# Masked maxima of the scores ahead of the keys' additions on VectorE, and all probabilities scaled on ScalarE

## The chip, the cores and the metric

One core of one Trainium2 chip runs the whole program. The metric is device time in microseconds (us) of one execution; smaller is better. The kernel before took 485.41 us, the median of three runs (484.21 to 485.72).

## The reference

A decoder trunk of two layers over 256 tokens with 1024 channels, all in float32. Layer 0 mixes tokens by attention with 8 heads of 128 channels; at 256 tokens there is one key block, so it is plain causal attention. Layer 1 mixes them by causal pooling. Each layer is followed by a squared-ReLU MLP with 4096 hidden channels, and a last RMSNorm closes the trunk.

```python
qkv = (xn @ w_qkv).reshape(b, s, 3, N_HEADS, HEAD_DIM)
q = apply_partial_rope(q, cos, sin)          # the first 32 channels of each head
k = apply_partial_rope(k, cos, sin)
s_own = jnp.einsum('bhqd,bhkd->bhqk', qc, k_own) * scale
s_own = jnp.where(kpos[None, :] <= qpos[:, None], s_own, NEG_INF)
p = jax.nn.softmax(s_own, axis=-1)
out = einsum('bhqk,bhkd->bhqd', p, v) @ w_o
x = x + out
x = x + squared_relu_mlp(rms_norm(x, norm_mlp[i]), w_up, w_down)   # relu(x @ w_up)**2 @ w_down
```

## The kernel before

Weights arrive from memory in slabs of 1 MB, `slabs`, in the order of their use: values, then keys and queries of two heads in turn, the output projection, and the MLP. Every slab is split into a high and a low part of reduced width: ScalarE copies the high part (`hi`, L177), VectorE subtracts it from the slab (`lo`, L181, "the split"). Most slabs have two pieces of 128 x 1024. The splits run about three slabs ahead of their use, and calls such as `pump_h(1)` and `pump(1)` place them among the other work. Products are then made of three matrix products of parts, summed in PSUM.

The order of work on every engine is written out by hand: an engine executes its instructions in the order in which the program gives them, and an instruction that waits holds all behind it on its engine.

The attention stage runs over `j`, pairs of heads, from 0 to 3 (L716 to L756). For `j` of 1 to 3, TensorE makes the keys of pair `j` in two banks (`wide_lo`, then `attend(j - 2)`, then `wide_hi`), then the scores of pair `j - 1` (L636, L637), then the queries of pair `j` (L410 to L415, some 5.9 us), then transposes the probabilities of pair `j - 1` (`prob_t`, L670). So each of these three blocks holds on the other engines:

- `key_evac` (L609): for both heads ScalarE copies the half of the bank with the small terms (L615) and VectorE adds the other half (L616, "the additions"); VectorE shuffles the 32 rotary channels (L617); GpSimd does the rotation in three operations (L620, L621, L622).
- `scores` (L629): VectorE adds the causal mask to each piece of the scores and takes the maximum of it in one instruction (L640, "the maxima": two pieces for each of the two heads); ScalarE makes a high part (L177) and then the four exponentials with their sums (L648); VectorE makes one split and then the reciprocals of the four sums (L651); then the probabilities are scaled, the first head's two pieces on ScalarE (L656), the second head's two on VectorE (L659).
- `qk_evac` (L593): VectorE shuffles (L598) and multiplies (L599) the queries; the rest is on VectorE for `j` = 1 and on GpSimd for `j` = 2 and 3 (L601, L602).
- `attend(j - 2)` (L688): the attention output of an earlier pair is copied by ScalarE (L709) and its low part is made by VectorE (L710).

The scores of pair 3 have no keys beside them: `scores(3)` stands among the output projection (L773).

The scores, transposed probabilities and attention outputs share one ring of two PSUM banks (`ps_t`, tag "t"). In the order of allocation, the second head's scores of pairs 1, 2 and 3 (`s_1_1`, `s_2_1`, `s_3_1`) come to the bank that the attention output of pair 0, 1 and 2 (`o_0`, `o_1`, `o_2`) had. TensorE therefore can't load for these scores before L710 of that pair has read the bank.

Of the kernel before, what the change touches and what calls it, by code (L numbers as in the profile page):

```python
# [11 lines left out]
F32 = mybir.dt.float32  # L12
F32R = mybir.dt.float32r
I32 = mybir.dt.int32
AF = mybir.ActivationFunctionType
ALU = mybir.AluOpType
ENG = mybir.EngineType

P = 128
SEQ = 256  # L20
# [64 lines left out]
def tile_trunk(ctx: ExitStack, tc: tile.TileContext, x_in, positions, norm_mix, norm_mlp,  # L85
               w_qkv, w_o, pool_w, pool_scale, w_up, w_down, norm_final, consts, out):
    nc = tc.nc
# [5 lines left out]
    work = ctx.enter_context(tc.tile_pool(name="work", bufs=2))  # L93
# [93 lines left out]
    def hi_step():  # L187

        if not todo:
            i = state["next"]  # L190
            if i > min(state["cur"] + AHEAD, len(slabs) - 1):
                return False
            todo.extend(split_steps(i))
            state["next"] += 1
        step = todo.pop(0)
        step[0]()
        lows.append((state["next"] - 1, not todo, step[1]))
        return True
# [11 lines left out]
    def pump_h(n):  # L210
        for _ in range(n):
            hi_step()

    def pump_l(n):
        for _ in range(n):
            lo_step()
# [7 lines left out]
    def use(kind, j, pieces=99):  # L224

        i = index[(kind, j)]
        state["cur"] = max(state["cur"], i)
        while done.get(i, 0) < pieces:
            if not lo_step():
                hi_step()  # L230
        wh, wl = halves[i]
        kk = slabs[i][1].shape[1]
        return (wh.rearrange("p (k f) -> p k f", k=kk), wl.rearrange("p (k f) -> p k f", k=kk))
# [184 lines left out]
    def chan_block(acc, w, f):  # L418
        for k in range(KT):
            chan_hi(acc, w, k, f, k == 0)  # L420
            chan_lo(acc, w, k, f, k == KT - 1)

    def wide_lo(acc, w, k, f, first=True):

        nc.tensor.matmul(acc[:, 0:SEQ], w[1][:, k, f * P:(f + 1) * P], xs[:, k, 0:SEQ],  # L425
                         start=first and k == 0, stop=not first and k == KT - 1,
                         skip_group_check=True)
# [79 lines left out]
    for k in range(KT):  # L507
# [29 lines left out]
        if 2 <= k < 6:  # L537
# [3 lines left out]
                                 scale=1.0 / 32.0, accum_out=acc0[:, h, s:s + 1])  # L541
        if k == 5:
# [4 lines left out]
                                           op0=ALU.add, op1=ALU.add)  # L547
# [22 lines left out]
    def v_evac(s, h):  # L570
        nc.scalar.activation(vsb[:, s, h * HALF:(h + 1) * HALF], dv[s, h], AF.Copy, scale=r0[s])
# [5 lines left out]
    scale = 1.0 / math.sqrt(P)  # L577
    tab = {}

    def tables():  # L580
        for nm, c in (("k", 1.0), ("q", scale)):
            ct = cpool.tile([P, 1, SEQ], F32, name="ct_" + nm)
            st = cpool.tile([ROT, 1, SEQ], F32, name="st_" + nm)
            nc.vector.scalar_tensor_tensor(ct[:, 0, :], rb[:, 0:SEQ], c, cos_t, op0=ALU.mult, op1=ALU.mult)
            nc.vector.scalar_tensor_tensor(st[:, 0, :], rb[0:ROT, 0:SEQ], c, sin_t, op0=ALU.mult, op1=ALU.mult)
            tab[nm] = (ct, st)
# [3 lines left out]
    def qk_bank(nm, j):  # L590
        return ps_u.tile([P, HALF], F32, tag="u", name="u_%s_%d" % (nm, j))

    def qk_evac(nm, j, u):  # L593
        ct, st = tab[nm]
        t = work.tile([P, 2, SEQ], F32, tag="X", name="t_%s_%d" % (nm, j), bufs=4)
        sw = work.tile([ROT, 2, SEQ], F32, tag="sw", name="sw_%s_%d" % (nm, j), bufs=2)
        uv = u.rearrange("p (f t) -> p f t", f=2)
        nc.vector.stream_shuffle(sw.rearrange("p f t -> p (f t)"), u[0:ROT, :], swap)  # L598
        nc.vector.tensor_tensor(t, uv, ct.broadcast_to([P, 2, SEQ]), op=ALU.mult)  # L599
        e = nc.vector if j == 0 or (nm, j) == ("q", 1) else nc.gpsimd  # L600
        e.tensor_tensor(sw, sw, st.broadcast_to([ROT, 2, SEQ]), op=ALU.mult)  # L601
        e.tensor_tensor(t[0:ROT], t[0:ROT], sw, op=ALU.add)  # L602
        return t

    def key_banks(j):
        return [ps_d.tile([P, HALF], F32, tag="d%d%d" % (f, 1 - j % 2), name="k_%d_%d" % (j, f))
                for f in range(2)]

    def key_evac(j, us):  # L609

        ct, st = tab["k"]
        t = work.tile([P, 2, SEQ], F32, tag="X", name="t_k_%d" % j, bufs=4)
        sw = work.tile([ROT, 2, SEQ], F32, tag="sw", name="sw_k_%d" % j, bufs=2)
        for f in range(2):
            nc.scalar.activation(t[:, f, :], us[f][:, SEQ:2 * SEQ], AF.Copy)  # L615
            nc.vector.tensor_tensor(t[:, f, :], us[f][:, 0:SEQ], t[:, f, :], op=ALU.add)  # L616
        nc.vector.stream_shuffle(sw.rearrange("p f t -> p (f t)"),  # L617
                                 t[0:ROT].rearrange("p f t -> p (f t)"), swap)
        e = nc.gpsimd
        e.tensor_tensor(t, t, ct.broadcast_to([P, 2, SEQ]), op=ALU.mult)  # L620
        e.tensor_tensor(sw, sw, st.broadcast_to([ROT, 2, SEQ]), op=ALU.mult)  # L621
        e.tensor_tensor(t[0:ROT], t[0:ROT], sw, op=ALU.add)  # L622
        return t

    qk = {}
    prob = {}
    mask = cst[:, C_MASK:C_MASK + 3 * P]

    def scores(j):  # L629
        q, k = qk["q", j], qk["k", j]  # L630
        pr = []
        mx = small.tile([P, 4], F32, tag="mx", name="mx_%d" % j)
        sums = small.tile([P, 4], F32, tag="sums", name="sums_%d" % j)
        for a in range(2):
            sp = ps_t.tile([P, HALF], F32, tag="t", name="s_%d_%d" % (j, a))
            nc.tensor.matmul(sp[:, 0:P], q[:, a, 0:P], k[:, a, 0:P], start=True, stop=True)  # L636
            nc.tensor.matmul(sp[:, P:3 * P], q[:, a, P:2 * P], k[:, a, :], start=True, stop=True)  # L637
            pa = work.tile([P, 3 * P], F32, tag="Y", name="p_%d_%d" % (j, a), bufs=4)
            for b, (c0, c1) in enumerate(((0, P), (P, 3 * P))):
                nc.vector.tensor_tensor_reduce(  # L640
                    pa[:, c0:c1], sp[:, c0:c1], mask[:, c0:c1], scale=-1.0, scalar=-NEG,
                    op0=ALU.add, op1=ALU.min, accum_out=mx[:, 2 * a + b:2 * a + b + 1])
            pr.append(pa)
        pump_h(1)
        for a in range(2):
            for b, (c0, c1) in enumerate(((0, P), (P, 3 * P))):
                i = 2 * a + b
                nc.scalar.activation(pr[a][:, c0:c1], pr[a][:, c0:c1], AF.Exp, scale=-1.0,  # L648
                                     bias=mx[:, i:i + 1], accum_out=sums[:, i:i + 1])
        pump_l(1)  # L650
        nc.vector.reciprocal(sums, sums)  # L651
        for a in range(2):
            for b, (c0, c1) in enumerate(((0, P), (P, 3 * P))):
                i = 2 * a + b
                if a == 0:
                    nc.scalar.activation(pr[a][:, c0:c1], pr[a][:, c0:c1], AF.Copy,  # L656
                                         scale=sums[:, i:i + 1])
                else:
                    nc.vector.tensor_scalar(pr[a][:, c0:c1], pr[a][:, c0:c1],  # L659
                                            sums[:, i:i + 1], None, op0=ALU.mult)  # L660
        prob[j] = pr

    pts = {}
# [52 lines left out]
    for j in range(4):  # L716
        w = use("k", j)
        if j == 0:
            u = qk_bank("k", j)
            chan_block(u, w, 0)  # L720
            tables()
            pump_h(2)
            v_evac(0, 0)
            v_evac(1, 0)
            chan_block(u, w, 1)
            v_evac(0, 1)
            v_evac(1, 1)
            qk["k", j] = qk_evac("k", j, u)
            pump_l(2)
        else:  # L730
            us = key_banks(j)
            for f in range(2):
                for k in range(KT):
                    wide_lo(us[f], w, k, f)
            pump(1)
            if j >= 2:
                attend(j - 2)
            for f in range(2):
                for k in range(KT):
                    wide_hi(us[f], w, k, f)  # L740
            qk["k", j] = key_evac(j, us)
            scores(j - 1)
        w = use("q", j)
        u = qk_bank("q", j)
        chan_block(u, w, 0)
        pump(1 if j else 2)
        chan_block(u, w, 1)
        qk["q", j] = qk_evac("q", j, u)
        if j == 0:
            pump(1)  # L750
        if j == 3:
            nc.scalar.activation(vh, vsb[:, 0, HALF:D], AF.Copy)
            nc.vector.tensor_tensor(vl, vsb[:, 0, HALF:D], vh.bitcast(F32), op=ALU.subtract)
        if j >= 1:
            prob_t(j - 1)
        pump(1)  # L756
# [437 lines left out]
```

## Time and profile before

| what | value |
|---|---|
| median of three runs | 485.41 us (484.21 to 485.72) |
| profiled execution | 484.62 us, span of the profile 482.5 us |
| TensorE matmuls (PE) | 474.7 us busy, 98% of the span |
| VectorE (DVE) | 338.8 us, 70% |
| ScalarE (ACT) | 255.1 us, 53% |
| GpSimd (POOL) | 43.1 us, 9% |
| TensorE clock granted in 44 to 108 us | 1.00 of full speed |

The span is the time from the first to the last instruction in the trace; the execution's own time has 2.1 us more around it. All times below are microseconds from the start of the span. The three blocks of the attention stage that the change touches begin with TensorE's keys at 42.1, 55.4 and 70.0.

### The profile page before, as it was taken

How to read it: one execution, taken by the hardware profiler on the slowest of the kernel's cores; microseconds unless marked ns; L12 is line 12 of the kernel's file. 1: busy time of each engine (PE TensorE's matmuls, PEld its weight loads, DVE VectorE, ACT ScalarE, POOL GpSimd, SP SyncE). 2: the span in 40 equal slices, each digit the busy share in tenths (PEclk: the TensorE clock that was granted, in tenths of full speed). 3: DMA queues.
4: the chain of work that ended last, by engine and by line, in shares of the span. 5: the costliest groups of instructions: out<-in, count | busy, mean ns of one | idle time of the engine just before them, and what ended most of it. 6: DMA issues, size and time to landing. Idle time of an engine off the chain costs nothing.

```text
span 482.5 us, 6552 instructions
## 1 busy us (share of the span) xinstructions
PE 474.7 (98%) x2570; PEld 412.1 (85%) x2570; DVE 338.8 (70%) x498; ACT 255.1 (53%) x418; POOL 43.1 (9%) x41
## 2 busy tenths in 40 slices
PE   8999999999999999999999999999999999999994
PEld 7789999888888888888888889888888888888884
DVE  4789998955877484848566687778756557484745
ACT  4696665653686272635355554476535446272523
POOL 6910456300000000000000000000000000000000
PEclk9999999999999999999999999999999999999999
DMA  7986643480477758556573570078747472736202
GB/s 266 349 280 223 196 174 123 143 259 1 124 251 236 263 196 282 186 163 219 170 249 147 175 261 2 18 248 297 239 135 277 139 252 97 262 120 230 88 1 87
DMA packets 57342, 89.58 MB, mean 186 GB/s; under 512 B 2944, under 2 KB 46048, under 8 KB 57312
## 3 DMA queue, kind: packets, MB, share of 16 engines
q1 hardware_dynamic: 56896, 88.72, 55.1%
q8 instruction: 20, 0.33, 0.3%
q10 hardware_dynamic: 416, 0.45, 0.3%
q14 instruction: 10, 0.08, 0.0%
HBM read 88.11 MB, written 1.05 MB: 185 GB/s over the span
## 4 chain that ended last, share of the span: by engine, by line
PE 97%; DMA 1%; SPq 0%; ACT 0%; DVE 0%; issue 0%; ACTq 0%
PE u_m L432 24%; PE u_m L425 13%; PE d_m L401 12%; PE d_m L402 12%; PE d_m L403 12%; PE d_v L520 4%; PE k L432 2%; PE u_q L411 2%; PE u_q L410 2%; PE u_q L415 2%; PE d_o L401 2%; PE d_o L403 2%; PE d_o L402 2%; DMA xt<-in_x_dram 1%; PE k L425 1%; PE d_p L1066 1%
## 5 line engine op out<-in xcount | busy, mean ns | idle before, releaser
L432 PE MATMUL u_m<-xs,wh_u 128*128 128x512 f32 x512 | 122.1, 390 | 0.0
L432 PEld LDWEIGHTS u_m<-xs,wh_u 128*128 128x128 f32 x512 | 94.7, 188 | 18.8
L401 PE MATMUL d_m<-wh_d,hh 128*128 128x512 f32 x252 | 98.1, 389 | 0.0
L402 PE MATMUL d_m<-wl_d,hh 128*128 128x512 f32 x252 | 98.0, 389 | 0.0
L403 PE MATMUL d_m<-wh_d,hl 128*128 128x512 f32 x252 | 98.0, 389 | 0.0
L181 DVE TENSOR_TENSOR wl_d<-raw_d,wh_d 128x1024 fp32r<-128x1024 f32 x64 | 76.2, 1221 | 17.0 <-ACT wh_d L177 17.0
L181 DVE TENSOR_TENSOR wl_u<-raw_u,wh_u 128x1024 fp32r<-128x1024 f32 x64 | 75.8, 1222 | 12.2 <-ACT wh_u L177 12.2
L177 ACT ACTIVATE wh_d<-raw_d 128x1024 fp32r<-128x1024 f32 x64 | 64.7, 1046 | 21.7 <-DMA raw_d<-in_mlp_w_down_dram 21.7
L799 ACT ACTIVATE t<-u_m 128x256 f32<-128x256 f32 x64 | 24.0, 378 | 83.8 <-PE u_m L425 54.6
L177 ACT ACTIVATE wh_u<-raw_u 128x1024 fp32r<-128x1024 f32 x64 | 63.9, 1046 | 7.1 <-DMA raw_u<-in_mlp_w_up_dram 7.1
L425 PEld LDWEIGHTS u_m<-xs,wl_u 128*128 128x128 f32 x512 | 64.0, 191 | 1.4
L425 PE MATMUL u_m<-xs,wl_u 128*128 128x256 f32 x512 | 64.9, 283 | 0.0
L800 DVE TENSOR_TENSOR t<-u_m,t 128x256 f32<-128x256 f32 x64 | 26.5, 422 | 53.9 <-ACT t L799 53.2
L403 PEld LDWEIGHTS d_m<-wh_d,hl 128*128 128x128 f32 x252 | 47.3, 188 | 9.8
L401 PEld LDWEIGHTS d_m<-wh_d,hh 128*128 128x128 f32 x252 | 47.3, 188 | 9.8
L402 PEld LDWEIGHTS d_m<-wl_d,hh 128*128 128x128 f32 x252 | 47.3, 188 | 9.8
L810 ACT ACTIVATE hh<-hf 128x512 fp32r<-128x512 f32 x32 | 20.2, 633 | 45.0 <-DVE hf L809 45.0
L811 DVE TENSOR_TENSOR hl<-hf,hh 128x512 fp32r<-128x512 f32 x32 | 22.2, 692 | 22.5 <-ACT hh L810 22.5
L809 DVE SCALAR_TENSOR_TENSOR hf<-t 128x512 f32<-128x512 f32 x32 | 22.1, 692 | 1.1
L410 PE MATMUL u_q<-xs,wh_q 128*128 128x256 f32 x64 | 18.6, 291 | 0.0
L411 PE MATMUL u_q<-xs,wl_q 128*128 128x256 f32 x64 | 18.1, 283 | 0.0
L415 PE MATMUL u_q<-xs,wh_q 128*128 128x256 f32 x64 | 18.1, 283 | 0.0
(218 smaller groups left out, 554.8 us busy)
## 6 DMA issues: line engine op xcount, KB each, us to landing
raw_u<-in_mlp_w_up_dram SPq DMA_DIRECT2D x32, 1024.0 KB, 6.3
raw_d<-in_mlp_w_down_dram SPq DMA_DIRECT2D x32, 1024.0 KB, 4.8
raw_o<-in_attn_w_o_dram SPq DMA_DIRECT2D x4, 1024.0 KB, 4.8
raw_k<-in_attn_w_qkv_dram SPq DMA_DIRECT2D x4, 768.0 KB, 5.2
raw_q<-in_attn_w_qkv_dram SPq DMA_DIRECT2D x4, 768.0 KB, 4.8
raw_v<-in_attn_w_qkv_dram SPq DMA_DIRECT2D x2, 1024.0 KB, 9.0
raw_v<-in_attn_w_qkv_dram SPq DMA_DIRECT2D x3, 512.0 KB, 7.1
raw_k<-in_attn_w_qkv_dram SPq DMA_DIRECT2D x4, 256.0 KB, 5.4
```

The costliest lines, as they stand in the source:

```text
L177: nc.scalar.activation(wh[:, sl], src[:, sl], AF.Copy)
L181: nc.vector.tensor_tensor(wl[:, sl], src[:, sl], wh[:, sl].bitcast(F32), op=ALU.subtract)
L401: nc.tensor.matmul(acc, lh, wh, start=first, stop=False)
L402: nc.tensor.matmul(acc, lh, wl, start=False, stop=False)
L403: nc.tensor.matmul(acc, ll, wh, start=False, stop=last)
L410: nc.tensor.matmul(o, w[0][:, k, fs], hi, start=first, stop=False, skip_group_check=True)
L411: nc.tensor.matmul(o, w[1][:, k, fs], hi, start=False, stop=False, skip_group_check=True)
L415: nc.tensor.matmul(acc[:, f * SEQ:(f + 1) * SEQ], w[0][:, k, fs], xs[:, k, SEQ:2 * SEQ], start=False, stop=last, skip_group_check=True)
L425: nc.tensor.matmul(acc[:, 0:SEQ], w[1][:, k, f * P:(f + 1) * P], xs[:, k, 0:SEQ], start=first and k == 0, stop=not first and k == KT - 1, ...
L432: nc.tensor.matmul(acc, w[0][:, k, f * P:(f + 1) * P], xs[:, k, :], start=first and k == 0, stop=not first and k == KT - 1, skip_group_che ...
L799: nc.scalar.activation(t[:, ts], u[:, SEQ:2 * SEQ], AF.Copy)
L800: nc.vector.tensor_tensor(t[:, ts], u[:, 0:SEQ], t[:, ts], op=ALU.add)
```

## The change

The copies of the small terms become a function of their own, `small_terms`, that is called before `scores`. The rest of `key_evac` (additions, shuffle, GpSimd's rotation) is handed to `scores` as `between` and is called after the four maxima instead of ahead of them. The order on TensorE and on ScalarE up to the exponentials is as before; on VectorE the maxima change places with the additions and the shuffle, and GpSimd's three operations follow the shuffle. At the end of `scores` all four pieces of the probabilities are scaled on ScalarE, in all four calls; VectorE's two instructions (L659) are gone.

```diff
+    def small_terms(nm, j, us):
+        t = work.tile([P, 2, SEQ], F32, tag="X", name="t_%s_%d" % (nm, j), bufs=4)
+        for f in range(2):
+            nc.scalar.activation(t[:, f, :], us[f][:, SEQ:2 * SEQ], AF.Copy)
+        return t
-    def key_evac(j, us):
+    def key_evac(j, us, t):
         ct, st = tab["k"]
-        t = work.tile([P, 2, SEQ], F32, tag="X", name="t_k_%d" % j, bufs=4)
         sw = work.tile([ROT, 2, SEQ], F32, tag="sw", name="sw_k_%d" % j, bufs=2)
         for f in range(2):
-            nc.scalar.activation(t[:, f, :], us[f][:, SEQ:2 * SEQ], AF.Copy)
             nc.vector.tensor_tensor(t[:, f, :], us[f][:, 0:SEQ], t[:, f, :], op=ALU.add)
...
-    def scores(j):
+    def scores(j, between=None):
...
             pr.append(pa)
+        if between is not None:
+            between()
         pump_h(1)
...
-                if a == 0:
-                    nc.scalar.activation(pr[a][:, c0:c1], pr[a][:, c0:c1], AF.Copy,
-                                         scale=sums[:, i:i + 1])
-                else:
-                    nc.vector.tensor_scalar(pr[a][:, c0:c1], pr[a][:, c0:c1],
-                                            sums[:, i:i + 1], None, op0=ALU.mult)
+                nc.scalar.activation(pr[a][:, c0:c1], pr[a][:, c0:c1], AF.Copy,
+                                     scale=sums[:, i:i + 1])
...
-            qk["k", j] = key_evac(j, us)
-            scores(j - 1)
+            t = small_terms("k", j, us)
+            scores(j - 1, lambda: qk.update({("k", j): key_evac(j, us, t)}))
```

## Rows read from the trace of the kernel before

**Rows 1.** Busy time by engine, sum over the windows 44:62, 62:78, 78:92, 92:108.

```profile
sum 64.00, PE 64.00 PEld 57.87 DVE 55.90 ACT 38.05 POOL 22.02; mean PE 16.00 PEld 14.47 DVE 13.97 ACT 9.51 POOL 5.51
```

**Rows 2.** Timeline, DVE, 49 to 63: start, duration, line, out<-in, count [idle before].

```profile
49.68 0.74 DVE L616 TENSOR_TENSOR t_k<-k,t_k 128x256 f32<-128x256 f32 x2
50.46 0.72 DVE L617 STREAM_SHUFFLE sw_k<-t_k 32x512 f32<-32x512 f32 x1
51.09 0.26 DVE L640 CUSTOM_DVE_ANT_0 p<-s,cst 128x128 f32<-128x128 f32 x1
...
52.18 1.46 DVE L181 TENSOR_TENSOR wl_q<-raw_q,wh_q 128x1024 fp32r<-128x1024 f32 x1
53.56 0.17 DVE L651 RECIPROCAL sums<-sums 128x4 f32<-128x4 f32 x1
53.77 1.38 DVE L659 TENSOR_SCALAR p<-p,sums 128x128 f32<-128x128 f32 x2
55.55 1.81 DVE L181 TENSOR_TENSOR wl_k<-raw_k,wh_k 128x1024 fp32r<-128x1024 f32 x1 [0.41 <-ACT wh_k L177]
...
57.29 0.72 DVE L598 STREAM_SHUFFLE sw_q<-u_q 32x512 f32<-32x512 f32 x1
...
62.09 0.67 DVE L710 TENSOR_TENSOR al<-o,ah 128x512 fp32r<-128x512 f32 x1
```

**Rows 3.** Timeline, DVE, the scaling of pair 3, with no GpSimd work beside it.

```profile
95.31 0.55 DVE L659 TENSOR_SCALAR p<-p,sums 128x128 f32<-128x128 f32 x2
```

**Rows 4.** Timeline, ACT, scaling of pair 0 and the high part behind it.

```profile
53.77 0.80 ACT L656 ACTIVATE p<-p,sums 128x128 f32<-128x128 f32 x2 [0.51 <-DVE sums L651]
54.47 1.04 ACT L177 ACTIVATE wh_k<-raw_k 128x1024 fp32r<-128x1024 f32 x1
```

**Rows 5.** Timeline, POOL, 51 to 73.

```profile
51.27 1.29 POOL L620 TENSOR_TENSOR t_k<-t_k,ct_k 128x512 f32<-128x512 f32 x1 [16.38 <-DVE sw_k L617]
...
54.86 1.41 POOL L622 TENSOR_TENSOR t_k<-t_k,sw_k 32x512 f32<-32x512 f32 x1
...
71.29 1.28 POOL L601 TENSOR_TENSOR sw_q<-sw_q,st_q 32x512 f32<-32x512 f32 x1 [1.83 <-DVE sw_q L598]
```

**Rows 6.** Timeline, POOL and DVE, two older pairs that start close together.

```profile
9.21 0.86 POOL L477 TENSOR_TENSOR rot_a<-rot_a,rot_b 32x256 f32<-32x256 f32 x1
9.41 1.22 DVE L181 TENSOR_TENSOR wl_v<-raw_v,wh_v 128x512 fp32r<-128x512 f32 x1
...
32.50 1.91 POOL L493 TENSOR_TENSOR rot_a<-rot_b 32x256 f32<-32x256 f32 x1 [8.58 <-ACT rot_b L491]
32.72 1.21 DVE L181 TENSOR_TENSOR wl_q<-raw_q,wh_q 128x1024 fp32r<-128x1024 f32 x1
```

**Rows 7.** Timeline, PEld and PE: the second head's scores of pairs 1, 2, 3.

```profile
62.82 0.39 PEld L636 LDWEIGHTS s<-t_k,t_q 128*128 128x128 f32 x2
63.24 0.60 PE L637 MATMUL s<-t_k,t_q 128*128 128x256 f32 x2
...
77.39 0.19 PEld L636 LDWEIGHTS s<-t_k,t_q 128*128 128x128 f32 x1
...
91.77 0.41 PEld L636 LDWEIGHTS s<-t_k,t_q 128*128 128x128 f32 x2
```

**Rows 8.** Timeline, DVE, the second and third block, 65 to 91.

```profile
65.30 1.52 DVE L181 TENSOR_TENSOR wl_q<-raw_q,wh_q 128x1024 fp32r<-128x1024 f32 x1
...
70.48 0.73 DVE L598 STREAM_SHUFFLE sw_q<-u_q 32x512 f32<-32x512 f32 x1
...
75.81 0.68 DVE L710 TENSOR_TENSOR al<-o,ah 128x512 fp32r<-128x512 f32 x1
...
79.86 1.51 DVE L181 TENSOR_TENSOR wl_o<-raw_o,wh_o 128x1024 fp32r<-128x1024 f32 x1
...
85.03 0.72 DVE L598 STREAM_SHUFFLE sw_q<-u_q 32x512 f32<-32x512 f32 x1
...
90.77 0.69 DVE L710 TENSOR_TENSOR al<-o,ah 128x512 fp32r<-128x512 f32 x1
```

## The prediction

> **What bounds the kernel now.** I read the busy time by stretch first, then the timelines of VectorE, ScalarE and GpSimd in the stretch that the change touches. In the windows from 44 to 108, TensorE is busy for all of the 64.00 us [rows 1]: it never waits there. Making another engine faster in this stretch therefore gives nothing. What can change the time is a new wait of TensorE, and nothing behind it gives it back, since TensorE fills 98% of the whole span too. So the question is which instruction that TensorE waits for has the least margin. The tightest is VectorE's L710. It frees the bank for the second head's scores. Before, it ends at 62.09 + 0.67 = 62.76, and TensorE loads for those scores at 62.82 [rows 2, 7]: 0.06 us later. In the next two blocks the same margin is 77.39 - (75.81 + 0.68) = 0.90 and 91.77 - (90.77 + 0.69) = 0.31 [rows 7, 8]. Each L710 stands at the end of a VectorE queue that runs nearly back to back, so a delay ahead of it arrives there whole.
>
> **A lock between VectorE and GpSimd.** The two scalings L659 of pair 0 take 1.38 us, those of pair 3, with GpSimd idle, 0.55 [rows 2, 3]. The split L181 takes 1.21 us alone [rows 6] but 1.46 and 1.81 beside GpSimd [rows 2]. GpSimd's last operation ends at 54.86 + 1.41 = 56.27, and the split that began at 55.55 ends 1.09 later, at 57.36 [rows 2, 5]. So these instructions don't overlap with GpSimd's: the later one waits to the end of the earlier one, and then needs some 0.13 less than alone. The other way round, that GpSimd operation waited for the scaling's end at 55.15 and ended 1.12 later, against 1.28 for one of its shape at 71.29 [rows 5].
>
> The Trainium skill ("SBUF — State Buffer", section "Who interferes with whom") states it as a rule: VectorE and GpSimd share a port pair, whoever issues first holds it for a whole instruction, and a VectorE instruction with two SBUF inputs contends too. The rows above agree. Read as shared bandwidth instead, the sum below would be near 0.
>
> **The change in the first block** (keys 1, scores 0).
> - *Swap.* Before, VectorE's additions start at 49.68, the shuffle at 50.46, the maxima at 51.09 and the split at 52.18 [rows 2]: 0.78, 0.63 and 1.09. After: maxima to 50.77, additions to 51.55, shuffle to 52.18, and the split starts at 52.18 again. The exponentials start 1.4 earlier but buy nothing, as the reciprocal stands behind the split.
> - *GpSimd.* Its first operation starts 0.81 after the shuffle's start [rows 2, 5], so at 52.36, now behind the split instead of 0.9 ahead of it. The split is unhindered: 1.21 instead of 1.46, end 53.39, reciprocal and scalings 0.25 earlier, at 53.52.
> - *Scalings.* Two on ScalarE take 0.70 up to the next instruction (53.77 to 54.47) [rows 4]; four take 1.40. The high part behind them starts at 54.92 instead of 54.47 (+0.45), and the split that waits for it at 56.00 instead of 55.55. The last probability is done at about 55.03 (the fourth piece takes some 0.5), VectorE's was at 55.15: the transposes don't suffer.
> - *Who is first at 56.00?* GpSimd's first operation is released at 53.39 and ends some 1.14 later (1.29 less the same 0.15), 54.53. The second finds the lock free: 1.28, end near 55.8. The third starts near 55.85, 0.15 ahead of the split. It takes 1.28, to 57.13, and the split ends 1.09 later, at 58.22 instead of 57.36: **+0.86**.
> - *What is behind.* From there VectorE's queue to L710 is as before, so L710 starts at 62.95 and ends at 63.62. TensorE loads 0.06 later, at 63.68 instead of 62.82: a new wait of **0.86**, with all of TensorE behind it.
>
> The lead of 0.15 is the one cost that no row shows, and it has two ends: 0 if the split goes first, 0.86 if GpSimd does. In the nearest row GpSimd, 0.20 ahead, held a 128x512 split to 1.22, as long as 1024 columns take alone. In the other, GpSimd's operation, 0.22 ahead but after 8.58 us of rest, waited and the split did not [rows 6]. Here GpSimd has just worked, as in the first; I take 0.86.
>
> **The second block** (keys 2, scores 1). The second head's scores end 63.24 + 0.60 + 0.86 = 64.70 [rows 7]. Its maxima (half of 1.09) follow, to 65.30, then the additions (0.78) and the shuffle (0.63): the split starts at 66.71 instead of 65.30 (+1.41) [rows 8]. Unhindered it takes 0.31 less (reciprocal +1.10); two more scalings make the high part +1.80; GpSimd's third operation is ahead of the next split by the same 0.15, which adds 0.86 - 0.45 = 0.41. The queries' shuffle is 2.21 late (70.48 before), and L710 with it: it ends at 78.70. TensorE would load at 77.39 + 0.86 = 78.25 and can at 78.76: **+0.51**, total 1.37.
>
> **The third block** (keys 3, scores 2), the same: scores end 78.76 + 1.02 = 79.78 (63.84 - 62.82 after the load), maxima 80.38, shuffle done 81.79, split +1.93 against 79.86; - 0.30 + 0.70 + 0.41 = 2.74 at the queries' shuffle (85.03 before) and at L710: end 90.77 + 2.74 + 0.69 = 94.20, load at 94.26. That is 2.49 after 91.77 [rows 7, 8], so the block adds **1.12**. Here attention also needs VectorE's parts of the probabilities on the way, but a wait for them is contained in the 2.49. The scores of pair 3 have no GpSimd work beside them, and their transposes come over 1 us after the probabilities; nothing is added. No DMA is moved past another in its queue, and each slab is split several us ahead of its use.
>
> **The sum.** 0.86 + 0.51 + 1.12 = 2.49 us on the profiled execution's 484.62 gives 487.1. The median of the runs is 0.79 above that execution; from it the forecast is 487.9. I put 487.4 between them. My own range for this case is +1.6 to +3.3, as each block's delay hangs on sums of some ten durations.
>
> **Rivals.**
> - *VectorE first (not slower).* If the split at 56.00 gets the lock ahead of GpSimd, it ends at 57.21, earlier than before, and the 0.86 is not there. The second block then is at most 0.45 late against a margin of 0.90, the third 0.45 against 0.31: about +0.15. That gives 484.8 to 485.6. It decides by 0.15 us of GpSimd's start, and "32.50 against 32.72" speaks for it.
> - *One wait alone.* The first block costs 0.86, but with everything shifted the order at the lock turns in the later blocks and their margins take the rest: +0.9, 485.5 to 486.3, within the bound of no change. Against it: the lead has the same parts in each block.
> - *Faster.* VectorE is rid of 1.38 us three times and the exponentials start earlier. It needs a wait of TensorE that this removes, of at least 1.46 us; the rows show none. Below 483.95.
>
> **How the numbers follow.** A measurement can tell about 0.3% of 485.41, 1.46 us, from no change. My case 0.57 (its lower tail stays within the bound), VectorE first 0.24, one wait alone 0.13, faster 0.04, more than my case 0.02. Slower by over 0.3%: 0.56; within: 0.40; faster: 0.04. The range from 484.6 to 488.7 takes in VectorE first for the most part, as the two ends of the unknown lead demand.
>
> **What would show it.** Right: idle time of TensorE ahead of L636, ended by VectorE's L710, in all three blocks, some 0.9, 0.5 and 1.1 (part of the last may stand ahead of L700); the split behind the scaling at 2.2 us instead of 1.81; GpSimd's third operation unhindered at 1.28. Wrong: that split at 1.2 and GpSimd's third operation longer (VectorE first), or TensorE still without a wait.

## The result, and the profile after

The changed kernel takes 488.14 us (median; 487.75 to 488.56) against 485.27 us for the kernel before: a ratio of 1.0064, 95% interval 1.0045 to 1.0082. A second comparison (e11 below) gave 1.0074 (1.0061 to 1.0086). So the change costs about 3 us; 487.4 was forecast, and 488.14 lies in the range.

The first view is the list of TensorE's waits in the changed kernel (in total, times, longest), without the one at the very start of the program. The kernel before has none of these three in its list.

```profile
PE o L695 <- DVE ptp L678: 0.9, 1, 0.9
PE s L640 <- POOL t_q L602: 0.9, 1, 0.9
PE s L640 <- DVE al L712: 0.6, 1, 0.6
```

The list counts only idle time after the modelled ends of matmuls. What TensorE really loses is read from the starts of its instructions. The rows are the first matmul of the keys of pair 1 and the first of the MLP, before and after.

```profile
42.11 0.28 PE L425 MATMUL k<-xs,wl_k 128*128 128x256 f32 x1
...
111.68 0.36 PE L425 MATMUL u_m<-xs,wl_u 128*128 128x256 f32 x1
```

```profile
42.10 0.28 PE L425 MATMUL k<-xs,wl_k 128*128 128x256 f32 x1
...
114.88 0.36 PE L425 MATMUL u_m<-xs,wl_u 128*128 128x256 f32 x1
```

I call the time between the two the stage: 69.57 us before, 72.78 after, so +3.2. From there to the last matmul the two kernels agree within 0.05 us. The work ahead of the stage, on the other hand, moves by up to 2.0 us from one profile to the next (the first of these matmuls starts between 41.35 and 43.33 in the profiles below), whatever the kernel. The stage is therefore the sharper measure of the two, and I give it beside each timed ratio.

The first block after, VectorE's timeline. (Lines have moved: L644 are the maxima, L620 the additions, L621 the shuffle, L657 the reciprocals, L661 the scalings, L712 what was L710, L624 to L626 GpSimd's three operations on the keys.)

```profile
49.69 0.27 DVE L644 CUSTOM_DVE_ANT_0 p<-s,cst 128x128 f32<-128x128 f32 x1
...
50.80 0.74 DVE L620 TENSOR_TENSOR t_k<-k,t_k 128x256 f32<-128x256 f32 x2
...
51.58 0.72 DVE L621 STREAM_SHUFFLE sw_k<-t_k 32x512 f32<-32x512 f32 x1
52.21 1.20 DVE L181 TENSOR_TENSOR wl_q<-raw_q,wh_q 128x1024 fp32r<-128x1024 f32 x1
53.33 0.16 DVE L657 RECIPROCAL sums<-sums 128x4 f32<-128x4 f32 x1
56.00 2.25 DVE L181 TENSOR_TENSOR wl_k<-raw_k,wh_k 128x1024 fp32r<-128x1024 f32 x1 [2.51 <-ACT wh_k L177]
...
58.19 0.72 DVE L598 STREAM_SHUFFLE sw_q<-u_q 32x512 f32<-32x512 f32 x1
...
62.99 0.67 DVE L712 TENSOR_TENSOR al<-o,ah 128x512 fp32r<-128x512 f32 x1
```

ScalarE and GpSimd beside it, and GpSimd in the second block (start, duration).

```profile
53.53 1.50 ACT L661 ACTIVATE p<-p,sums 128x128 f32<-128x128 f32 x4 [1.66 <-DVE sums L657]
54.93 1.04 ACT L177 ACTIVATE wh_k<-raw_k 128x1024 fp32r<-128x1024 f32 x1
```

```profile
52.38 2.18 POOL L624 TENSOR_TENSOR t_k<-t_k,ct_k 128x512 f32<-128x512 f32 x1 [17.56 <-DVE sw_k L621]
54.52 1.28 POOL L625 TENSOR_TENSOR sw_k<-sw_k,st_k 32x512 f32<-32x512 f32 x1
55.88 1.28 POOL L626 TENSOR_TENSOR t_k<-t_k,sw_k 32x512 f32<-32x512 f32 x1
...
70.45 1.28 POOL L626 TENSOR_TENSOR t_k<-t_k,sw_k 32x512 f32<-32x512 f32 x1
73.54 3.92 POOL L601 TENSOR_TENSOR sw_q<-sw_q,st_q 32x512 f32<-32x512 f32 x1 [1.81 <-DVE sw_q L598]
77.54 1.26 POOL L602 TENSOR_TENSOR t_q<-t_q,sw_q 32x512 f32<-32x512 f32 x1
```

Read the row at 56.00 against the one at 55.88: VectorE's split starts 0.12 us behind GpSimd's third operation, stands until that ends at 57.16, and takes 2.25 instead of 1.81 us [rows 2]. Everything behind it, down to L712, is 0.9 us later than before (62.99 against 62.09). TensorE's loads that wait, in the order of time:

```profile
63.71 0.30 PEld L640 LDWEIGHTS s<-t_k,t_q 128*128 128x128 f32 x2 [1.03 <-DVE al L712]
...
78.85 0.30 PEld L640 LDWEIGHTS s<-t_k,t_q 128*128 128x128 f32 x2 [1.36 <-POOL t_q L602]
```

```profile
91.91 0.71 PE L695 MATMUL o<-pts,vsb 128*128 128x128 f32 x4 [0.95 <-DVE ptp L678]
```

The starts of TensorE's instructions against those of before fall back by 0.8 to 0.9 us at the first, 1.20 at the second and 1.22 at the third.

### The profile page after: what moved, and what is told of

Its sections match the earlier page's. It is cut to its first block, busy times and chain, and to the rows that moved or that the text cites. A ratio compares the mean times of both kernels' runs of the same rounds, so it can differ in the third digit from the quotient of the medians.

```text
span 485.7 us, 6558 instructions
## 1 busy us (share of the span) xinstructions
PE 475.8 (98%) x2570; PEld 412.4 (85%) x2570; DVE 331.7 (68%) x490; ACT 257.6 (53%) x426; POOL 43.9 (9%) x41
## 4 chain that ended last, share of the span: by engine, by line
PE 89%; DVE 6%; ACT 1%; issue 1%; POOL 1%; DMA 1%; DVEq 0%; ACTq 0%
PE u_m L432 24%; PE u_m L425 13%; PE d_m L402 12%; PE d_m L403 12%; PE d_m L401 12%; PE d_v L520 5%; DVE wl_k L181 2%; PE d_o L401 1%; PE d_o L403 1%; PE d_o L402 1%; DVE wl_q L181 1%; DMA raw_q<-in_attn_w_qkv_dram 1%; POOL sw_q L601 1%; PE d_p L1068 1%; PE pb L985 1%
```

## The experiments

Two theories went into them. Theory A is that of the prediction: the swap moves GpSimd's operations into VectorE's later work, one engine holds the other up, and VectorE's or GpSimd's late results make TensorE wait. Theory B: the two scalings more on ScalarE make its high parts late, and all else follows.

| run | ratio to before (95%) | stage, change against 69.57 us |
|---|---|---|
| changed again (e11) | 1.0074 (1.0061 to 1.0086) | +3.2 |
| e1 swap only | 1.0021 (1.0012 to 1.0030) | +0.85 |
| e2 scalings only | 1.0007 (0.9998 to 1.0015) | +0.1 |
| e3 no third operation | 1.0001 (0.9991 to 1.0010) | +0.1 |
| e4 early high part | 1.0005 (0.9996 to 1.0014) | +0.2 |
| e5 other banks | 1.0053 (1.0037 to 1.0070) | +2.6 |
| e6 VectorE delayed | 1.0061 (1.0046 to 1.0076) | +2.5 |
| e7 block 1 alone | 1.0016 (1.0007 to 1.0026) | +0.8 |
| e8 L710 delayed | 1.0027 (1.0015 to 1.0038) | +1.3 |
| e9 GpSimd pause | 1.0005 (0.9996 to 1.0014) | +0.1 |
| e10 block 3 alone | 1.0027 (1.0017 to 1.0037) | +1.2 |
| e12 block 2 alone | 1.0024 (1.0012 to 1.0035) | +1.2 |

**e11, the changed kernel again,** with no edit, timed together with e9 and e10.

> The changed kernel once more, beside the kernel before on the same chip: +2.5 to +3.3 us, and the same three waits of TensorE in the profile (at the scores of pair 1, the scores of pair 2 and the attention of pair 2).

Its ratio and its stage agree with those of the first comparison, so 3 us is the size to be explained.

**e1, the swap alone; e2, the scalings alone.**

```diff
 # e1: the changed kernel with
+                if a == 0: nc.scalar.activation(...)
+                else: nc.vector.tensor_scalar(...)
 # e2: the kernel before with all four scalings on ScalarE
```

> Only the order is changed (maxima ahead of the keys' additions); the second head's probabilities stay on VectorE. Theory A (the lock: GpSimd's rotation now runs beside VectorE's later work, and what VectorE makes late keeps TensorE waiting): as slow as the full change or slower, +2.0 to +3.8 us over the kernel before, as the scalings on VectorE meet GpSimd too and may hold the transposes. Theory B (the longer row of scalings on ScalarE makes the high part late, and all else follows): no difference to the kernel before, within 0.3 us.

> Only the scalings are moved to ScalarE; the order on VectorE is that of before. Theory A: the split behind the scalings starts some 0.7 late but finds GpSimd's third operation done, so it ends within 0.15 of before: 0 to +0.3 us over the kernel before. Theory B: most of the loss, +1.5 to +3 us.

Neither half costs what both cost together: 0.85 + 0.1 against 3.2. Theory B is out by e2: the later high part alone costs next to nothing. But theory A's number for e1 was wrong too. The rows say why; VectorE, GpSimd and TensorE of e1:

```profile
53.34 2.41 DVE L665 TENSOR_SCALAR p<-p,sums 128x128 f32<-128x128 f32 x2
55.68 1.21 DVE L181 TENSOR_TENSOR wl_k<-raw_k,wh_k 128x1024 fp32r<-128x1024 f32 x1
```

```profile
54.34 1.26 POOL L625 TENSOR_TENSOR sw_k<-sw_k,st_k 32x512 f32<-32x512 f32 x1
55.68 2.36 POOL L626 TENSOR_TENSOR t_k<-t_k,sw_k 32x512 f32<-32x512 f32 x1
```

```profile
55.81 0.20 PEld L676 LDWEIGHTS pt<-ident,p 128*128 128x128 f32 x2 [0.91 <-DVE p L665]
```

The scalings on VectorE stand 2.41 us beside GpSimd and make the transposes late: that is the 0.85, nearly all of it in the first block. The high part on ScalarE is done at 55.09 here, ahead of the scalings' end, so the split starts right behind the scalings, in the same hundredth as GpSimd's third operation, 55.68. Here VectorE goes first: split 1.21, GpSimd 2.36. All later waits are gone. In e2, where GpSimd has its order of before, the third operation is done at 55.71 and the split at 55.80 takes 1.23:

```profile
54.43 1.28 POOL L622 TENSOR_TENSOR t_k<-t_k,sw_k 32x512 f32<-32x512 f32 x1
```

```profile
55.80 1.23 DVE L181 TENSOR_TENSOR wl_k<-raw_k,wh_k 128x1024 fp32r<-128x1024 f32 x1 [2.51 <-ACT wh_k L177]
```

So the swap delays GpSimd, the scalings delay the split, and only both together put the one right ahead of the other.

**e3, GpSimd's third operation left out; e9, GpSimd paused ahead of it.**

```diff
 # e3
-        e.tensor_tensor(t[0:ROT], t[0:ROT], sw, op=ALU.add)
 # e9
+        for _ in range(3):
+            e.memset(ones, 1.0)
         e.tensor_tensor(t[0:ROT], t[0:ROT], sw, op=ALU.add)
```

> The changed kernel without GpSimd's third operation on the keys of pairs 1 to 3 (the sum of the rotated channels is left out). Theory A: the split behind the scalings takes 1.2 us instead of 2.25, TensorE's wait at the scores of pair 1 is gone, and 0 to +0.8 us over the kernel before is left. Theory B: that split is as late as in the changed kernel since the scalings are, and the time stays at +2.8 to +3.2.

> The changed kernel with three more instructions on GpSimd (filling a 128x128 tile with the value that it holds, 0.2 us each) between its second and third operation on the keys. Theory A: in the changed kernel the third operation starts 0.12 us ahead of VectorE's split and holds it for over a us; with 0.4 us or more of delay it starts behind the split, the split takes 1.2 us, TensorE's three waits go or nearly go, and 0 to +0.6 us over the kernel before is left. Rival (the keys' rotation and the high part are late as such, whoever goes first): no gain, or up to 0.6 us slower than the changed kernel.

Both confirm theory A. In e3 the split takes 1.23 us (from 56.87). e9 is the sharper: it does more work than the changed kernel, in the same order, and is 3 us faster. Its rows, GpSimd and VectorE:

```profile
55.13 0.72 POOL L627 MEMSET ones<- 128x128 f32 x3
55.81 1.92 POOL L628 TENSOR_TENSOR t_k<-t_k,sw_k 32x512 f32<-32x512 f32 x1
```

```profile
55.38 1.22 DVE L181 TENSOR_TENSOR wl_k<-raw_k,wh_k 128x1024 fp32r<-128x1024 f32 x1 [2.51 <-ACT wh_k L177]
...
61.34 0.67 DVE L714 TENSOR_TENSOR al<-o,ah 128x512 fp32r<-128x512 f32 x1
```

The split has started first, takes 1.22, and GpSimd waits instead, on keys that TensorE first loads at 61.42, 3.7 us after they are done. TensorE's list has no wait left in the stage.

**e4, the high part made earlier.** ScalarE stands idle for 1.66 us ahead of the scalings (row at 53.53 above); the high part fits in there.

```diff
         pump_l(1)
+        if between is not None:
+            pump_h(1)
         nc.vector.reciprocal(sums, sums)
...
-        pump(1 if j else 2)
+        if j: pump_l(1)
+        else: pump(2)
```

> The changed kernel, but ScalarE makes the high part right behind the exponentials, while it waits for the reciprocals, instead of behind the scalings; its split then stands directly behind the reciprocals, ahead of GpSimd's second operation. Both theories: the waits of TensorE go, -0.2 to +0.5 us against the kernel before. If instead the swap by itself costs the time (keys rotated later), it stays at +2 to +3 us.

Right: 1.0005, no wait of TensorE left in the stage. This order costs nothing, but gains nothing either: before the change TensorE had no wait here that could be removed.

**e7, e12 and e10, one block alone.** The other blocks have the order and the scalings of before.

```diff
+            if j in (1,):      # e7; (2,) in e12, (3,) in e10
+                scores(j - 1, lambda: ...)
+            else:
+                qk["k", j] = key_evac(j, us, t); scores(j - 1)
```

> The change in the first block alone (keys 1 beside scores 0); the other blocks as before. TensorE waits once, 0.9 us, at the second head's scores of pair 1; since TensorE is then late itself, nothing is added later: +0.8 to +1.0 us over the kernel before. If the delay is carried on by VectorE, +1.5 or more.

> The change in the second block alone (keys 2 beside scores 1). VectorE's shuffle of the queries of pair 2 is some 1.4 us late. If GpSimd's first operation on these queries loses the lock to the two splits behind it, as in the changed kernel, TensorE waits some 1.0 us for the rotated queries at the scores of pair 2; if it gets the lock, some 0.5 us for L710. In all +0.5 to +1.2 us over the kernel before, so that the three blocks alone add to about the 3.2 us of the full change. If the second wait of the changed kernel needs the lateness of the first block, +0 to +0.3.

> The change in the third block alone (keys 3 beside scores 2). Theory A, with the second head's scores in time: GpSimd's third operation is ahead of the split again; VectorE's shuffle of the queries is some 1.4 us late; TensorE waits once, at the attention of pair 2 or the scores of pair 3: +0.9 to +1.3 us over the kernel before. If the third wait of the changed kernel only comes from lateness that the first two blocks hand on, +0 to +0.4.

All three came as expected, e12 at the upper end of its range. Each block makes one wait of TensorE, the same as in the full change: for L710 in e7, and these in e12 and e10 (from the lists of TensorE's waits, the line numbers their own):

```profile
PE s L640 <- POOL t_q L602: 0.9, 1, 0.9
```

```profile
PE o L699 <- DVE ptp L682: 1.0, 1, 1.0
```

In the stage they cost 0.8 + 1.2 + 1.2 = 3.2 us, which is the whole. So the blocks don't hand their lateness on: a wait of TensorE in one block moves all of the next with it.

**e8, L710 of pair 0 made late in the kernel before.**

```diff
         nc.scalar.activation(ah[:, 2 * j:2 * j + 2, :], ov, AF.Copy)
+        for _ in range(6 if late else 0):
+            nc.vector.memset(warm, 0.0)
```

> The kernel before with six more instructions on VectorE (clearing an unused 128x128 tile) right ahead of L710 of pair 0, 0.6 to 0.9 us in all. If the margin of 0.06 us is real, TensorE waits ahead of the second head's scores of pair 1 for as long as L710 is late less 0.06, and the time grows by it, +0.5 to +0.9 us. If TensorE has hidden slack there, no change.

The six took more than I had put (0.26 us from one to the next), so the size missed. The margin is as small as predicted: L710 (here L712) ends at 64.54, 1.40 us later in the stage than before, and the stage is 1.3 us longer. The wait in the list:

```profile
PE s L636 <- DVE al L712: 1.0, 1, 1.0
```

**e5, other banks for the scores.**

```diff
-            sp = ps_t.tile([P, HALF], F32, tag="t", ...)
+            sp = ps_d.tile([P, HALF], F32, tag="d%d%d" % (a, (j + 1) % 2), ...)   # pairs 0 to 2
```

> The changed kernel with the scores of pairs 0 to 2 in the two banks that the previous keys have left, so that they don't wait for L710 (here L712) of an earlier pair. Theory A (the late queue of VectorE and GpSimd is what counts, and the bank is only where TensorE meets it first): the first wait of 0.9 us goes, but about half of it comes back at the next meeting point; +1.5 to +2.7 us over the kernel before in all. Rival (the wait for the bank is the root, and the later waits follow from it): +0 to +1.2.

The first wait is gone from the list, the other two stay, and the next one has grown; the gain is 0.6 us of 3.2:

```profile
PE s L643 <- POOL t_q L602: 1.3, 1, 1.3
PE o L698 <- DVE ptp L681: 1.0, 1, 1.0
```

The bank is only where TensorE meets the late queue first.

**e6, VectorE delayed behind the queries of pair 2.**

```diff
         qk["q", j] = qk_evac("q", j, u)
+        if j == 2:
+            nc.vector.memset(warm, 0.0)
+            nc.vector.memset(warm, 0.0)
```

> The changed kernel with two more instructions on VectorE (clearing an unused 128x128 tile, some 0.1 us each) behind the queries of pair 2, ahead of two splits. Theory A with a late start of GpSimd after a rest: GpSimd's first operation on these queries now leads the split by some 0.65 instead of 0.42 us, gets the lock, and takes 1.3 instead of 3.9; TensorE's wait at the scores of pair 2 falls from 1.2 to some 0.6, and the time by 0.3 to 0.8 us against the changed kernel. Rival (VectorE's queue alone counts): 0.2 us slower than the changed kernel.

In the profile it came as theory A has it. GpSimd's first operation on the queries now starts 0.81 ahead of the splits, and takes 1.28 where it took 3.92; the splits wait instead:

```profile
74.77 1.28 POOL L601 TENSOR_TENSOR sw_q<-sw_q,st_q 32x512 f32<-32x512 f32 x1 [1.81 <-DVE sw_q L598]
76.13 2.15 POOL L602 TENSOR_TENSOR t_q<-t_q,sw_q 32x512 f32<-32x512 f32 x1
```

```profile
75.58 3.79 DVE L181 TENSOR_TENSOR wl_o<-raw_o,wh_o 128x1024 fp32r<-128x1024 f32 x2
79.29 0.68 DVE L712 TENSOR_TENSOR al<-o,ah 128x512 fp32r<-128x512 f32 x1
```

TensorE's wait there is now for L712 and costs 0.5 us instead of 1.2, which is the second block as it had been predicted, and the stage is 0.7 us shorter than with the full change. In the timed runs the two can't be told apart: 1.0061 against 1.0064 and 1.0074, with intervals that overlap. For e6 the profile alone is the evidence.

## Why the prediction was right, and where it was not

- *TensorE without a wait, so only a new wait counts.* Right. The stage took all of the change, and nothing behind it gave any back.
- *The swap, the scalings, the lock in the first block.* Right nearly to the hundredth: split at 52.21 (52.18 predicted), scalings at 53.53 (53.52), high part at 54.93 (54.92), GpSimd's third operation at 55.88 (55.85), the split behind it at 56.00 (56.00) with its end at 58.25 (58.22), TensorE's load at 63.71 (63.68).
- *Who goes first when GpSimd leads by 0.15.* It led by 0.12 and went first, in all three blocks. This was the one cost that no row showed. e9 and e1 show the other side: when the split starts no later, VectorE goes first. The rival "VectorE first" thus has its mechanism right and names the right point. e9 lands near its price (+0.1 of the stage, +0.15 predicted), but at another place: TensorE loads for the scores of pair 2 some 0.1 late, behind GpSimd's rotation of the queries (L602), and not in the third block.
- *The second block.* Here the step failed that let L710 follow the queries' shuffle as it did before ("a delay ahead of it arrives there whole", "and L710 with it"). The shuffle came at 72.74 (72.69 predicted; the maxima ahead of it took 0.56, where the sum has 0.60 for half of 1.09). But the queue behind the shuffle held waits of its own: before, GpSimd's first operation on the queries ran ahead of two splits [rows 5], and these took 4.09 us. After, that order turned. GpSimd's operation, 0.42 us ahead of the split, did not get its turn until both splits were through, and took 3.92 us. VectorE gained by that, before and after:

```profile
71.80 4.09 DVE L181 TENSOR_TENSOR wl_o<-raw_o,wh_o 128x1024 fp32r<-128x1024 f32 x2
```

```profile
73.96 2.34 DVE L181 TENSOR_TENSOR wl_o<-raw_o,wh_o 128x1024 fp32r<-128x1024 f32 x2
76.23 0.67 DVE L712 TENSOR_TENSOR al<-o,ah 128x512 fp32r<-128x512 f32 x1
```

  L712 was only 0.42 late instead of 2.21, and the queries of pair 2 came last, at 78.80: 1.20 us instead of 0.51. This is nearly the whole miss of the sum (3.2 against 2.49).
- *The third block.* The size was right, 1.22 against 1.12, but the place was one that the prediction had left as a possibility for a part of it: TensorE waits for VectorE's parts of the probabilities (L678, which free the bank of `o_2`), a little ahead of L712.
- *Sign and chances.* "Slower by over 0.3%" had 0.56; the measured 0.6% lies above the bound with all of its interval. "One wait alone" had the lock turn in later blocks, as it did, but took for granted that a turn relieves TensorE; it moved the wait to GpSimd's result.

The Trainium skill's rule on the shared port ("SBUF — State Buffer", "Who interferes with whom") gives the pair to whoever issues first, for a whole instruction, and the other is blocked. The first block and e9 agree: the one that starts first holds, the other waits in full. In e1 the recorded starts are equal, and there too one waits in full for the other. The second block differs, going by recorded starts: GpSimd started 0.42 us ahead of the split, at 73.54, and still waited for two splits in a row.

## What to carry to other kernels

Where the engine that sets the time has no wait in a stretch, moving work between the others can only lose there: list first which of their results has the least margin, here 0.06 us, and price the change by what arrives there. Two edits that cost little one by one (+0.85 and +0.1) can meet: look at what each does to the start of instructions that exclude one another, here VectorE's splits and scalings and GpSimd's operations. When two such starts come to lie within some tenths of a us, give the lead on purpose to the one that something waits for, by an earlier issue (e4) or by holding the other back (e9), and read from the next profile who went first.

## What the runs showed of the hardware that was not expected

- A lead in the recorded starts does not by itself say who goes first. Right behind its own work, GpSimd went first with 0.11 to 0.12 us (55.88 against 56.00, 70.45 against 70.56). After 1.8 us of rest it lost with 0.42 us (73.54 against 73.96; the same in e11 and e12), and won with 0.81 (e6). But in the second block of e7 it won with 0.41 us after the same rest, and the two splits waited:

```profile
72.02 1.27 POOL L601 TENSOR_TENSOR sw_q<-sw_q,st_q 32x512 f32<-32x512 f32 x1 [1.83 <-DVE sw_q L598]
```

```profile
72.43 4.17 DVE L181 TENSOR_TENSOR wl_o<-raw_o,wh_o 128x1024 fp32r<-128x1024 f32 x2
```

  e8 shows the same with 0.43. So neither the lead nor the time of rest decides here, and why the order turned in the second block stays open.
- A GpSimd operation that has lost can wait for VectorE's next split too: 3.92 us for an operation of 1.28, with two splits that follow without a gap. In other places a waiting GpSimd operation got its turn between two splits (2.15 us in e6, at 76.13). What decides between the two is open; no run here was made to tell it.
